# One power for both halves of a projection's head scales in a hybrid attention layer

## The chip, the cores and the metric

The kernel runs on one core of one Trainium2 chip. The metric is device time in microseconds, the median of several executions. Weights, inputs and outputs are float32; every large product is made of three float32r products (high by high, high by low, low by high).

## The reference

One decoder layer over 512 tokens with 1024 columns: a half-step SwiGLU, then two attention branches from one combined projection, then a second half-step SwiGLU. What matters for the change is that queries and keys are normalized per head before use:

```python
def rms_norm(x, g):
    y = xf * lax.rsqrt(jnp.mean(xf * xf, axis=-1, keepdims=True) + EPS)
    return (y * g).astype(x.dtype)

fq = rms_norm(fq.reshape(B, S, 8, 64), fox_q_norm)   # branch A: queries, keys
fk = rms_norm(fk.reshape(B, S, 8, 64), fox_k_norm)
dq = rms_norm(dq.reshape(B, S, 8, 64), dsa_q_norm)   # branch B: queries
dk = rms_norm(dk, dsa_k_norm)                        # one shared key head
```

Branch A is causal attention of 8 heads with a bias from cumulated forget gates. Branch B chooses for each query the 128 best keys by an indexer and attends to those, 8 query heads on one shared key and value head, with a position bias.

## The kernel before

Tokens stand in four blocks of 128 (`NT = 4`). The first feed-forward half-step takes the first 350 us, the second the last 320 us. Between them the projections are `units` of matmuls, and the attention loop runs over 16 heads `g` (0 to 7 branch A, 8 to 15 branch B) with four steps `s` each; at step `s` the scores of token block `i = 3 - s` are made, with 128(i+1) columns. `prod.run` fills TensorE between the steps with matmuls of pending units. TensorE's order is written out by hand. In this stage the orders of VectorE (DVE), ScalarE (ACT), GpSimd (POOL) and the DMA queue (SP) come from a scheduler that estimates when each operation is ready; every engine then works through its own list strictly in order.

A projection of keys or queries is one unit, `tm_proj`, of 256 columns: four heads for each of the four token blocks. Its result lies in two PSUM tiles, one for two token blocks each; these are the two halves `b` of `normed` (line 954). Six projections go through it: `fk0`, `fq0`, `fk1`, `fq1`, `dq0`, `dq1`. For each half, ACT copies PSUM to the tile `kn` (line 961, two instructions), ACT squares it into `sqh` (L857), DVE sums over the 64 columns of a head into `ss` (L859, 8 sums: two blocks of four heads), DVE scales and adds EPS (L860), POOL raises to the power -0.5 against the tile `nhalf` into `rh` (L862), and POOL multiplies `kn` by it (L964). `qk_scale` holds the middle four. `dsa_keys` calls it too, once for each token block with a single head, for the shared sparse key.

A normalized projection is used some time later: `get_k` and `get_q` transpose pairs of heads on TensorE (`ps_k`, `ps_q`, L868), and ACT and DVE take them apart into high and low parts (`kh` L851, `kl` L852, `st` L881 and L882). `ps_k`, `ps_q` and the transposed probabilities `pt` (L1209) share two PSUM banks (tag `pt`).

One step of the attention loop is, engine by engine: POOL makes the bias `b` (L1272, in branch B L1276) and masks its last 128 columns (AFFINE_SELECT, L1273); TensorE makes the score `ps_qk` (L890, L891), in one of two banks (tag `s`); DVE adds bias and score and takes the minimum (L1198, with its result `p` and `mn`); ACT takes the exponential and the row sum (L1200); DVE inverts the sum (`rs`, L1201); POOL multiplies `p` by it (L1202). The probabilities of a head are then flipped (`pt`), split by ACT into `ph` (L1213) and by DVE into `pl` (L1214), and multiplied with the values into `po` (L1219, L1220). At a head's end ACT copies `po` out twice (L1226, L1229), POOL adds the two (`o`, L1230), ACT and DVE split the sum (L1233, L1234). Values go from PSUM to `fv` by ACT (L974) and DVE (L975). Weights are split by ACT (`wh`, L138) and DVE (`wl`, L144), or, for ten of the chunks, by an accumulating DMA that POOL issues (L142).

Of the kernel before, what the change touches and what calls it, by code (L numbers as in the profile page):

```python
# [12 lines left out]
F32 = mybir.dt.float32  # L13
F32R = mybir.dt.float32r
AF = mybir.ActivationFunctionType
OP = mybir.AluOpType
AX = mybir.AxisListType
PSUM = bass.MemoryType.PSUM

P = 128  # L20
T = 512
NT = T // P
# [14 lines left out]
H = 8  # L37
DH = 64
TOPK = 128
EPS = 1e-6  # L40
# [15 lines left out]
def tile_hybrid_layer(ctx: ExitStack, tc: tile.TileContext, a: dict):  # L56
    nc = tc.nc
    V, S, G, PE = nc.vector, nc.scalar, nc.gpsimd, nc.tensor

    ctx.enter_context(tc.manual_schedule(engines={mybir.EngineType.PE}))  # L60
    const = ctx.enter_context(tc.tile_pool(name="const", bufs=1))
# [3 lines left out]
    small = ctx.enter_context(tc.tile_pool(name="small", bufs=4))  # L65
# [5 lines left out]
    def tmp_tile(name):  # L71
        return tmp.tile([P, T], F32, tag="t", name=name)
# [6 lines left out]
    for _ in range(WARM):  # L79
# [8 lines left out]
    G.memset(cpos, 0.0)  # L88
    G.affine_select(out=cpos, in_=cpos, compare_op=OP.is_ge, fill=BIG, base=0,
                    pattern=[[-1, P]], channel_multiplier=1)  # L90
    nhalf = const.tile([P, 8], F32, name="nhalf")
    G.memset(nhalf, -0.5)

    gains = const.tile([P, 3, KD], F32, name="gains")
# [671 lines left out]
    with tc.tile_pool(name="begin", bufs=1) as bp, tc.manual_schedule(  # L766
# [21 lines left out]
        for nm in ("w_gate1", "w_up1"):  # L788
            tag = next(raw_tags)
# [41 lines left out]
    with (tc.tile_pool(name="mix", bufs=1) as mp, ExitStack() as att_ctx,  # L831
# [7 lines left out]
        sd = [at.tile([P, NT, 2, DH], F32, tag="cb", bufs=2, name="sd") for _ in range(2)]  # L839
# [10 lines left out]
        def evac_split(ps, g, hi, lo):  # L850
            S.mul(hi, ps, g)  # L851
            V.scalar_tensor_tensor(lo, ps, g, hi.bitcast(F32), op0=OP.mult, op1=OP.subtract)  # L852

        def qk_scale(src, nh):

            sq = tmp_tile("sqh")
            S.activation(sq[:, :nh * DH], src, AF.Square)  # L857
            ss = small.tile([P, 8], F32, tag="ss", name="ss")
            V.tensor_reduce(ss[:, :nh], sq[:, :nh * DH].rearrange("p (h d) -> p h d", d=DH), axis=AX.X, op=OP.add)  # L859
            V.tensor_scalar(ss[:, :nh], ss[:, :nh], 1.0 / DH, EPS, op0=OP.mult, op1=OP.add)  # L860
            r = small.tile([P, 8], F32, tag="rh", name="rh")
            G.tensor_tensor(r[:, :nh], ss[:, :nh], nhalf[:, :nh], op=OP.pow)  # L862
            return r

        def transposed(cols, name):
            ps = psum.tile([P, T], F32, tag="pt", bufs=2, name=name)
            for t in range(NT):
                PE.transpose(ps[:, t * P:(t + 1) * P], cols(t), ident)  # L868
            return ps
# [83 lines left out]

        def normed(key):
            def done(ps):
                out = []
                for b in range(2):
                    kn = mp.tile([P, T], F32, tag="tn", bufs=8, name="kn")
                    kv = kn.rearrange("p (u c) -> p u c", u=2)
                    for u in range(2):  # L960
                        S.mul(kv[:, u], ps[b][:, u], rt[:, 2 * b + u:2 * b + u + 1])
                    r = qk_scale(kn, H)
                    kh = kn.rearrange("p (h d) -> p h d", d=DH)
                    G.tensor_mul(kh, kh, r[:, :, None].to_broadcast([P, H, DH]))  # L964
                    out.append(kv)
                tn[key] = out
            return done

# [128 lines left out]
        V.tensor_sub(ikl, ps, ikh.bitcast(F32))  # L1097

        def dsa_keys():
            for t in range(NT):  # L1100
                r = qk_scale(sd[0][:, t, 0], 1)
                V.tensor_scalar(sd[0][:, t], sd[0][:, t], r[:, 0:1], None, op0=OP.mult)
                S.copy(dvv[:, t, 0:64], sg[:, t, 0:64])
                V.tensor_sub(dvv[:, t, 64:128], sg[:, t, 0:64], dvv[:, t, 0:64].bitcast(F32))
            yield
            evac_split(transposed(lambda t: sd[0][:, t].rearrange("p a d -> p (a d)"), "ps_dk"), hg[:, 3:4], dkh, dkl)
# [63 lines left out]
        for h in range(H):  # L1170
# [3 lines left out]
            for i in range(1, NT):  # L1174
# [4 lines left out]
                r = tmp_tile("relu")  # L1179
# [5 lines left out]
                if h == H - 1:  # L1185
                    V.tensor_sub(sc[i][:, n - P:n], sc[i][:, n - P:n], cpos)
        later = [dsa_keys(), forget()]
        for g in later:
            next(g)
# [291 lines left out]
```

## Time and profile before

| | |
|---|---|
| median of 3 runs | 1066.27 us (1066.22 to 1066.71) |
| the profiled execution | 1065.68 us |
| its span, first to last instruction | 1064.0 us |
| TensorE busy | 1050.9 us, granted clock 1.000 |
| DVE, ACT, POOL busy | 849.9, 672.5, 258.9 us |

All times inside the program are in microseconds from the start of the span. A row of the order of time gives start, duration, engine, line, operation, output and inputs, and shapes; in brackets stands how long the engine was idle before it and which operation ended that. A row with xN merges N like instructions that follow each other. A row of the groups ends with busy time in all, the mean duration in nanoseconds, the idle time before and what ended it. What looks like full TensorE use is made of overlapping matmuls, so the small idle times are what a change of the other engines can add to or take from.

### The profile page before, as it was taken

The numbers are of one execution on the slowest core, as the hardware profiler recorded it, in microseconds if no ns is written. First come the engines' busy times: TensorE is split into PE (matmuls) and PEld (weight loads), VectorE is DVE, ScalarE is ACT, GpSimd is POOL, SyncE is SP. The second block draws the span as 40 slices with busy tenths as digits, with TensorE's granted clock in tenths as the row PEclk, the third lists the DMA queues.
The fourth block names the chain that finished last, engine by engine and source line by source line (L and its number), as shares of the span: only waits on it lengthen the run. The fifth ranks groups of instructions, "written<-read, shape, count | busy, mean of one in ns | idle before, by whom it ended". The sixth has DMA issues, their size and how long they took to land.

```text
span 1064.0 us, 19526 instructions
## 1 busy us (share of the span) xinstructions
PE 1050.9 (99%) x7438; PEld 978.0 (92%) x7438; DVE 849.9 (80%) x1400; ACT 672.5 (63%) x1120; POOL 258.9 (24%) x325
## 2 busy tenths in 40 slices
PE   9999999999999999999999999999999999999998
PEld 6889999999999899999877788888889999999998
DVE  6987888897889689976777765854987888887887
ACT  6736765765777675576867665433736765775673
POOL 1100211120122024277776653000100210111111
PEclk9999999999999999999999999999999999999999
DMA  7644654666557358633223321532543665567554
GB/s 244 150 151 115 154 155 134 143 160 174 125 126 180 99 136 201 190 92 107 80 61 119 119 70 50 162 125 78 129 160 99 148 154 156 130 158 186 127 125 129
DMA packets 57917, 143.71 MB, mean 135 GB/s; under 512 B 6616, under 2 KB 15960, under 8 KB 57824
## 3 DMA queue, kind: packets, MB, share of 16 engines
q1 hardware_dynamic: 39888, 110.22, 33.6%
q0 software_dynamic: 17792, 31.99, 17.1%
q8 instruction: 58, 0.95, 0.4%
q10 hardware_dynamic: 144, 0.26, 0.1%
q14 instruction: 35, 0.29, 0.1%
HBM read 104.94 MB, written 3.42 MB: 102 GB/s over the span
## 4 chain that ended last, share of the span: by engine, by line
PE 89%; DVE 3%; POOL 3%; ACT 2%; issue 2%; DMA 1%; SPq 0%; DVEq 0%; POOLq 0%; ACTq 0%
PE pB L149 5%; PE pB L151 5%; PE pB L150 5%; PE pA L149 3%; PE pA L151 3%; PE pA L150 3%; PE ps_f L149 3%; PE ps_f L151 3%; PE ps_f L150 3%; PE dB L151 2%; PE dB L149 2%; PE dB L150 2%; PE ps_t L149 2%; PE ps_t L151 2%; PE ps_t L150 2%; PE dA L150 2%
## 5 line engine op out<-in xcount | busy, mean ns | idle before, releaser
L118 ACT CAST wh<-s 128x1024 fp32r<-128x1024 f32 (+1 forms) x90 | 86.8, 965 | 65.6 <-PE pC L150 33.0
L125 DVE TENSOR_TENSOR wl<-s,wh 128x1024 fp32r<-128x1024 f32 (+1 forms) x90 | 100.3, 1114 | 26.9 <-ACT wh L118 26.9
L149 PE MATMUL ps_t<-wh,xh 128*128 128x256 f32 (+1 forms) x288 | 80.7, 280 | 0.0
L149 PE MATMUL pB<-tbh,wh 128*128 128x256 f32 x288 | 80.4, 279 | 0.0
L150 PE MATMUL pB<-tbl,wh 128*128 128x256 f32 x288 | 80.4, 279 | 0.0
L151 PE MATMUL ps_t<-wh,xl 128*128 128x256 f32 (+1 forms) x288 | 80.4, 279 | 0.0
L151 PE MATMUL pB<-tbh,wl 128*128 128x256 f32 x288 | 80.3, 279 | 0.0
L150 PE MATMUL ps_t<-wl,xh 128*128 128x256 f32 (+1 forms) x288 | 80.1, 278 | 0.0
L243 POOL DMA_DIRECT2D b<-gu x12 | 10.4, 864 | 222.2 <-DVE rf L443 98.4
L149 PE MATMUL ps_f<-xh,wh 128*128 128x512 f32 x152 | 60.5, 398 | 0.0
L151 PE MATMUL ps_f<-xh,wl 128*128 128x512 f32 x152 | 59.6, 392 | 0.0
L150 PE MATMUL ps_f<-xl,wh 128*128 128x512 f32 x152 | 59.6, 392 | 0.0
L1202 POOL TENSOR_SCALAR p<-p,rs 128x512 f32<-128x512 f32 (+1 forms) x64 | 40.3, 633 | 59.3 <-DVE rs L1201 57.3
L150 PEld LDWEIGHTS ps_t<-wl,xh 128*128 128x128 f32 x288 | 54.3, 188 | 0.4
L149 PEld LDWEIGHTS ps_t<-wh,xh 128*128 128x128 f32 x288 | 54.3, 188 | 0.4
L151 PEld LDWEIGHTS ps_t<-wh,xl 128*128 128x128 f32 x288 | 54.3, 188 | 0.0
L150 PEld LDWEIGHTS pB<-tbl,wh 128*128 128x128 f32 x288 | 54.1, 188 | 0.0
L151 PEld LDWEIGHTS pB<-tbh,wl 128*128 128x128 f32 x288 | 54.1, 188 | 0.0
L149 PEld LDWEIGHTS pB<-tbh,wh 128*128 128x128 f32 x288 | 54.1, 188 | 0.0
L569 POOL DMA_DIRECT2D xa<-e x20 | 23.9, 1241 | 122.5 <-ACT wh L118 102.8
L1200 ACT ACTIVATE p<-p,mn 128x512 f32<-128x512 f32 (+1 forms) x64 | 35.9, 562 | 25.1 <-DVE mn L1198 24.8
L1214 DVE TENSOR_TENSOR pl<-pt,ph 128x512 fp32r<-128x512 f32 (+1 forms) x64 | 31.0, 486 | 19.7 <-ACT ph L1213 19.0
(406 smaller groups left out, 4203.8 us busy)
## 6 DMA issues: line engine op xcount, KB each, us to landing
ra<-in_w_pair_dram SPq DMA_DIRECT2D x15, 512.0 KB, 3.9
rc<-in_w_pair_dram SPq DMA_DIRECT2D x15, 512.0 KB, 4.1
re<-in_w_pair_dram SPq DMA_DIRECT2D x12, 512.0 KB, 3.6
rf<-in_w_pair_dram SPq DMA_DIRECT2D x12, 512.0 KB, 3.5
rb<-in_w_pair_dram SPq DMA_DIRECT2D x12, 512.0 KB, 3.6
xa<-e POOLq DMA_DIRECT2D x22, 256.0 KB, 4.3
rd<-in_w_halves_dram SPq DMA_DIRECT2D x12, 384.0 KB, 3.9
ra<-in_w_halves_dram SPq DMA_DIRECT2D x9, 384.0 KB, 3.3
```

The lines of the kernel that those rows point to most:

```text
L118: S.copy(wh[:, :f], raw[:, :f])
L125: V.tensor_sub(wl[:, :f], raw[:, :f], wh[:, :f].bitcast(F32))
L149: PE.matmul(out, lh, rh, start=start, stop=False, **more)
L150: PE.matmul(out, lh, rl, start=False, stop=False, **more)
L151: PE.matmul(out, ll, rh, start=False, stop=stop, **more)
L243: G.dma_start(l, src, accum_op=OP.add)
L569: G.dma_start(xa[:, d:d + 2, HT:], t["e"][part], accum_op=OP.add)
L1200: S.activation(p, p, AF.Exp, bias=mn, scale=-1.0, accum_out=rs)
L1202: G.tensor_scalar(p, p, rs, 1.0, op0=OP.mult, op1=OP.mult)
L1214: V.tensor_sub(pl[:, sl], pt[:, sl], ph[:, sl].bitcast(F32))
```

## The change

`qk_scale` goes. In `normed`, both halves are copied, squared and summed first, into one tile `ss` of 2 x 8; one correction, one power with 16 columns and then the two multiplies follow. `dsa_keys` squares, sums, corrects and raises all four token blocks in one instruction each. `nhalf` grows from 8 to 16 columns, and the new tiles `ss2` and `rh2` have one buffer. TensorE's order is the same, and the arithmetic of each value is the same.

```diff
-    nhalf = const.tile([P, 8], F32, name="nhalf")
+    nhalf = const.tile([P, 2 * H], F32, name="nhalf")
...
-        def qk_scale(src, nh):
-            sq = tmp_tile("sqh")
-            S.activation(sq[:, :nh * DH], src, AF.Square)
-            ss = small.tile([P, 8], F32, tag="ss", name="ss")
-            V.tensor_reduce(ss[:, :nh], sq[:, :nh * DH].rearrange("p (h d) -> p h d", d=DH), axis=AX.X, op=OP.add)
-            V.tensor_scalar(ss[:, :nh], ss[:, :nh], 1.0 / DH, EPS, op0=OP.mult, op1=OP.add)
-            r = small.tile([P, 8], F32, tag="rh", name="rh")
-            G.tensor_tensor(r[:, :nh], ss[:, :nh], nhalf[:, :nh], op=OP.pow)
-            return r
...
         def normed(key):
             def done(ps):
-                out = []
+                out, kns = [], []
+                ss = small.tile([P, 2, H], F32, tag="ss2", bufs=1, name="ss")
                 for b in range(2):
                     kn = mp.tile([P, T], F32, tag="tn", bufs=8, name="kn")
                     kv = kn.rearrange("p (u c) -> p u c", u=2)
                     for u in range(2):
                         S.mul(kv[:, u], ps[b][:, u], rt[:, 2 * b + u:2 * b + u + 1])
-                    r = qk_scale(kn, H)
-                    kh = kn.rearrange("p (h d) -> p h d", d=DH)
-                    G.tensor_mul(kh, kh, r[:, :, None].to_broadcast([P, H, DH]))
+                    sq = tmp_tile("sqh")
+                    S.activation(sq, kn, AF.Square)
+                    V.tensor_reduce(ss[:, b], sq.rearrange("p (h d) -> p h d", d=DH), axis=AX.X, op=OP.add)
+                    kns.append(kn)
                     out.append(kv)
+                V.tensor_scalar(ss, ss, 1.0 / DH, EPS, op0=OP.mult, op1=OP.add)
+                r = small.tile([P, 2, H], F32, tag="rh2", bufs=1, name="rh")
+                G.tensor_tensor(r, ss, nhalf.rearrange("p (a h) -> p a h", a=2), op=OP.pow)
+                for b in range(2):
+                    kh = kns[b].rearrange("p (h d) -> p h d", d=DH)
+                    G.tensor_mul(kh, kh, r[:, b, :, None].to_broadcast([P, H, DH]))
                 tn[key] = out
             return done
...
         def dsa_keys():
+            sq = tmp_tile("sqh")
+            S.activation(sq[:, :NT * DH].rearrange("p (t d) -> p t d", t=NT), sd[0][:, :, 0], AF.Square)
+            ss = small.tile([P, 8], F32, tag="ss", name="ss")
+            V.tensor_reduce(ss[:, :NT], sq[:, :NT * DH].rearrange("p (t d) -> p t d", t=NT), axis=AX.X, op=OP.add)
+            V.tensor_scalar(ss[:, :NT], ss[:, :NT], 1.0 / DH, EPS, op0=OP.mult, op1=OP.add)
+            r = small.tile([P, 8], F32, tag="rh", bufs=2, name="rh")
+            G.tensor_tensor(r[:, :NT], ss[:, :NT], nhalf[:, :NT], op=OP.pow)
             for t in range(NT):
-                r = qk_scale(sd[0][:, t, 0], 1)
-                V.tensor_scalar(sd[0][:, t], sd[0][:, t], r[:, 0:1], None, op0=OP.mult)
+                V.tensor_scalar(sd[0][:, t], sd[0][:, t], r[:, t:t + 1], None, op0=OP.mult)
```

The scheduler answers with other orders on the four engines. In the changed file the lines of this stage have other numbers (POOL's power is L959, its multiply L962, `p` L1205, `b` L1275 and L1279, the mask L1276, `o` L1233). Three places follow.

POOL in head 3, while `fq1` is normalized: `rh` is the power, `kn` the multiply, `p` the normalized probabilities. Before:

```order
L1273 AFFINE_SELECT b<-b 128x128
L1230 TENSOR_TENSOR o<-o_5867,o 64x512
L862 TENSOR_TENSOR rh<-ss,nhalf 128x8
L1272 TENSOR_SCALAR b<-cb,ncum 128x256
L1272 TENSOR_SCALAR b<-cb,ncum 128x128
L1272 TENSOR_SCALAR b<-cb,ncum 128x512
L1202 TENSOR_SCALAR p<-p,rs 128x384
L964 TENSOR_TENSOR kn<-kn,rh 128x512
L1273 AFFINE_SELECT b<-b 128x128 x3
L862 TENSOR_TENSOR rh<-ss,nhalf 128x8
L964 TENSOR_TENSOR kn<-kn,rh 128x512
L1202 TENSOR_SCALAR p<-p,rs 128x256
```

And now:

```order
L1276 AFFINE_SELECT b<-b 128x128
L1233 TENSOR_TENSOR o<-o_5834,o 64x512
L1275 TENSOR_SCALAR b<-cb,ncum 128x256
L1275 TENSOR_SCALAR b<-cb,ncum 128x128
L1275 TENSOR_SCALAR b<-cb,ncum 128x512
L1276 AFFINE_SELECT b<-b 128x128
L1205 TENSOR_SCALAR p<-p,rs 128x384
L1276 AFFINE_SELECT b<-b 128x128 x2
L1205 TENSOR_SCALAR p<-p,rs 128x256
L959 TENSOR_TENSOR rh<-ss,nhalf 128x16
L1205 TENSOR_SCALAR p<-p,rs 128x128
L962 TENSOR_TENSOR kn<-kn,rh 128x512 x2
```

The first power and the first multiply have left the place ahead of the masks; the one power stands after `p` of 256 columns, and both multiplies after `p` of 128 columns.

ACT at the change from head 3 to head 4, where `get_k` splits the keys of the next heads. Before:

```order
L851 ACTIVATE kh<-ps_k,hg 64x512
L1213 CAST ph<-pt 128x512
L1226 COPY o<-po 64x512
L1229 COPY o_6097<-po 64x512
L851 ACTIVATE kh<-ps_k,hg 64x512
L974 ACTIVATE fv<-ps_t,rstd 128x4x64
L881 ACTIVATE st<-ps_q,gq 64x512
```

And now:

```order
L851 ACTIVATE kh<-ps_k,hg 64x512
L1216 CAST ph<-pt 128x512
L1229 COPY o<-po 64x512
L1232 COPY o_6060<-po 64x512
L971 ACTIVATE fv<-ps_t,rstd 128x4x64
L851 ACTIVATE kh<-ps_k,hg 64x512
L971 ACTIVATE fv<-ps_t,rstd 128x4x64
```

A copy of values `fv` stands ahead of the second `kh`; on DVE its partner stands ahead of the second `kl` in the same way.

POOL in head 7, while `dq1` is normalized. Before:

```order
L862 TENSOR_TENSOR rh<-ss,nhalf 128x8
L1202 TENSOR_SCALAR p<-p,rs 128x128
L964 TENSOR_TENSOR kn<-kn,rh 128x512
L1202 TENSOR_SCALAR p<-p,rs 128x512
L1272 TENSOR_SCALAR b<-cb,ncum 128x384
L1272 TENSOR_SCALAR b<-cb,ncum 128x256
L1272 TENSOR_SCALAR b<-cb,ncum 128x128
L1276 TENSOR_TENSOR b<-sc_4162,cb 128x512
L1273 AFFINE_SELECT b<-b 128x128
L1230 TENSOR_TENSOR o<-o_6881,o 64x512
L1273 AFFINE_SELECT b<-b 128x128 x2
```

And now:

```order
L959 TENSOR_TENSOR rh<-ss,nhalf 128x16
L1205 TENSOR_SCALAR p<-p,rs 128x128
L1205 TENSOR_SCALAR p<-p,rs 128x512
L962 TENSOR_TENSOR kn<-kn,rh 128x512 x2
L1275 TENSOR_SCALAR b<-cb,ncum 128x384
L1275 TENSOR_SCALAR b<-cb,ncum 128x256
L1275 TENSOR_SCALAR b<-cb,ncum 128x128
L1279 TENSOR_TENSOR b<-sc_4162,cb 128x512
L1233 TENSOR_TENSOR o<-o_6836,o 64x512
L1276 AFFINE_SELECT b<-b 128x128 x3
```

Both multiplies now stand behind `p` of 512 columns and ahead of the biases, and all three masks behind the addition `o`.

## The prediction

> **What bounds the kernel now.** I read the page first, then busy time by stretches, then the order of time on TensorE, and at each of its waits the order of time on the engine that is named there.
>
> ```profile
> span 1064.0 us, 19526 instructions
> PE 1050.9 (99%) x7438; PEld 978.0 (92%) x7438; DVE 849.9 (80%) x1400; ACT 672.5 (63%) x1120; POOL 258.9 (24%) x325
> ...
> 20.00:455.00 435.00, 434.99 (x3286) 415.59 (x3285) 372.17 (x615) 282.31 (x440) 76.00 (x86) 1.00 0.59 150
> 455.00:550.00 95.00, 90.29 (x661) 83.84 (x660) 69.39 (x171) 69.42 (x157) 73.59 (x106) 1.00 0.31 89
> 550.00:660.00 110.00, 107.24 (x554) 88.40 (x553) 78.50 (x182) 71.55 (x158) 62.95 (x74) 1.00 0.28 86
> ```
>
> The columns of the last three rows are the stretch, its length, then busy time of PE, weight loads, DVE, ACT and POOL. PE's work and its order stay as they are, so only its idle time can move: 0.01 us from 20 to 455, 4.71 us from 455 to 550, 2.76 us from 550 to 660. The rest (start and final drain) lies outside the edit. The changed operations run from 390 to 540, so what they can give directly is those 4.71 us. POOL's 24% is an average: it is busy for 73.59 of 95 us there.
>
> ```profile
> 432.03 0.28 PE L151 MATMUL ps_t<-wh,xl 128*128 128x256 f32 x1
> 432.15 0.60 PE L868 MATMUL ps_q<-ident,kn 128*128 128x128 f32 x4
> ...
> 482.73 0.50 PE L890 MATMUL ps_qk<-kh,st 128*128 128x512 f32 x1 [0.58 <-DVE mn L1198]
> 486.32 0.66 PE L1209 MATMUL pt<-ident,p 128*128 128x128 f32 x4 [0.32 <-POOL p L1202]
> 490.41 0.55 PE L1209 MATMUL pt<-ident,p 128*128 128x128 f32 x3 [0.31 <-DVE kl L852]
> ...
> 517.03 0.55 PE L1209 MATMUL pt<-ident,p 128*128 128x128 f32 x3 [1.06 <-DVE kl L852]
> ...
> 538.23 0.66 PE L1209 MATMUL pt<-ident,p 128*128 128x128 f32 x4 [1.07 <-POOL p L1202]
> ...
> 544.79 0.22 PE L890 MATMUL ps_qk<-kh,st 128*128 128x128 f32 x1
> 547.80 0.38 PE L1220 MATMUL po<-pl,fv 128*128 128x256 f32 x1 [0.33 <-DVE pl L1214]
> ```
>
> A matmul is drawn 0.28 long but the next starts 0.12 later (432.03, 432.15), so a stall costs about 0.16 more than the idle printed. I count 0.74, 0.48, 0.47, 1.22, 1.23 and 0.49 us for the six.
>
> **The price of one power.**
>
> ```profile
> L862 POOL TENSOR_TENSOR rh<-ss,nhalf 128x8 f32<-128x8 f32 x12 | 21.9, 1828 | 12.5 <-DVE ss L860 12.3
> L964 POOL TENSOR_TENSOR kn<-kn,rh 128x512 f32<-128x512 f32 x12 | 13.4, 1118 | 0.2
> L185 POOL TENSOR_TENSOR rstd<-v,nhalf 128x4 f32<-128x4 f32 x3 | 3.4, 1143 | 15.3 <-DVE v L183 15.2
> L862 POOL TENSOR_TENSOR rh<-ss,nhalf 128x1 f32<-128x1 f32 x4 | 2.5, 861 | 0.0
> L860 DVE TENSOR_SCALAR ss<-ss 128x8 f32<-128x8 f32 x12 | 3.1, 257 | 0.1
> ...
> 482.68 1.66 POOL L862 TENSOR_TENSOR rh<-ss,nhalf 128x8 f32<-128x8 f32 x1
> ```
>
> No row has 16 columns. Undisturbed, 8 cost 1.66 and 4 cost 1.14 (mean), 0.13 a column. 16 then cost 1.66 + 8 x 0.13 = 2.7 us (my value). The bounds are 1.66 (flat) and 3.32 (two for the price of two). Each projection saves 0.6 us of POOL, six of them 3.7. The sparse keys' four powers (2.5) become one of 1.14, and their four squares, sums and corrections become one each. That saving, and the six corrections dropped on DVE (about 0.26 each), lie up to 455 for the first two projections and the sparse keys, where PE idles 0.01 us and PE is the cover. I count them 0; later corrections sit beside DVE's own waits. With the cover gone they could give at most their own 2.5 us, which nothing on PE asks for.
>
> What the edit really moves is order: no power starts before the second half's sum, and two multiplies (1.12 each, mean) follow it in one piece.
>
> **First query projection (418 to 432): counted 0.**
>
> ```profile
> 424.91 1.66 POOL L862 TENSOR_TENSOR rh<-ss,nhalf 128x8 f32<-128x8 f32 x1 [1.84 <-DVE ss L860]
> ...
> 428.73 0.92 POOL L142 DMA_DIRECT2D wl<-ra  x1 [1.03 <-ACT wl L141]
> ```
>
> POOL's new order puts this weight transfer ahead of both multiplies, and it waits for ACT until 428.7. The power (424.9 to 427.6) is done by then. The multiplies run behind the transfer, which ends at 429.65: 2 x 1.12 gives 431.9, and PE takes them at 432.15 and after. It fits by 0.25 us; what comes later than that PE pays in full.
>
> **Head 3, POOL: -1.22 us.**
>
> ```profile
> 476.12 2.71 POOL L862 TENSOR_TENSOR rh<-ss,nhalf 128x8 f32<-128x8 f32 x1 [0.17 <-DVE ss L860]
> 478.84 1.55 POOL L1272 TENSOR_SCALAR b<-cb,ncum 128x256 f32<-128x256 f32 x3
> ...
> 481.92 0.80 POOL L1273 TENSOR_SCALAR_AFFINE_SELECT b<-b 128x128 f32<-128x128 f32 x3
> ...
> 485.45 1.49 POOL L1202 TENSOR_SCALAR p<-p,rs 128x256 f32<-128x256 f32 x3
> ...
> 482.24 0.43 DVE L1198 CUSTOM_DVE_ANT_0 p<-ps_qk,b 128x256 f32<-128x256 f32 x1 [1.83 <-POOL b L1273]
> 482.80 1.22 DVE L144 TENSOR_TENSOR wl<-rc,wh 128x1024 fp32r<-128x1024 f32 x1
> ```
>
> PE waits at 482.73 for DVE's score, the score for the mask (481.92), and the mask stands behind power, biases and multiply. In the new order the first power and multiply are gone from there: biases 476.1 to 477.7, mask by 478.0, over 4 us early. The 0.74 goes. Next, the wait at 486.32 is for p of 128 columns. The new queue is p256, power, p128, then the multiplies. With the power from about 481.5 to 484.2, p128 is ready at 484.6, and PE, 0.74 earlier, asks at about 485.2. The 0.48 goes too.
>
> [...]
>
> **Head 3 to 4, ACT: +0.5 us.**
>
> ```profile
> 489.59 0.47 ACT L974 ACTIVATE fv<-ps_t,rstd 128x256 fp32r<-128x256 f32 x1
> ...
> 489.60 0.76 DVE L852 SCALAR_TENSOR_TENSOR kl<-ps_k,hg,kh 64x512 fp32r<-64x512 f32 x1 [1.22 <-ACT kh L851]
> ```
>
> PE's transposes at 490.41 wait for the bank that this kl frees. The new order runs a value copy fv (0.47) ahead of that kh. Chain and demand both come 1.22 us earlier, so the wait grows by the copy: 0.47 to about 0.97.
>
> **Head 5, DVE: +0.2 us.**
>
> ```profile
> 515.18 0.67 DVE L860 TENSOR_SCALAR ss<-ss 128x8 f32<-128x8 f32 x1
> 516.22 0.76 DVE L852 SCALAR_TENSOR_TENSOR kl<-ps_k,hg,kh 64x512 fp32r<-64x512 f32 x1 [0.37 <-ACT kh L851]
> 517.01 0.56 DVE L1198 CUSTOM_DVE_ANT_0 p<-ps_qk,b 128x384 f32<-128x384 f32 x1
> ```
>
> The score of 517.01 now stands ahead of the kl of 516.22: 515.85 + 0.56 = 516.41, so kl starts 0.2 late and the 1.22 at 517.03 becomes 1.4.
>
> **Head 7, POOL: +0.8 us.**
>
> ```profile
> 536.15 1.66 POOL L862 TENSOR_TENSOR rh<-ss,nhalf 128x8 f32<-128x8 f32 x1
> 537.81 0.36 POOL L1202 TENSOR_SCALAR p<-p,rs 128x128 f32<-128x128 f32 x1
> ...
> 539.17 1.71 POOL L1202 TENSOR_SCALAR p<-p,rs 128x512 f32<-128x512 f32 x1
> 540.86 1.41 POOL L1272 TENSOR_SCALAR b<-cb,ncum 128x384 f32<-128x384 f32 x3
> ...
> 543.49 0.29 POOL L1273 TENSOR_SCALAR_AFFINE_SELECT b<-b 128x128 f32<-128x128 f32 x1
> 543.86 1.29 POOL L1230 TENSOR_TENSOR o<-o,o 64x512 f32<-64x512 f32 x1
> ...
> 543.81 0.56 DVE L1198 CUSTOM_DVE_ANT_0 p<-ps_qk,b 128x384 f32<-128x384 f32 x1 [0.45 <-POOL b L1273]
> ```
>
> The score of 128 columns no longer waits behind biases, so the power can start near 534.8 and p128 ends at 537.9 in place of 538.17: -0.3. Behind it now come p512 (1.71 here, about 0.7 inside the 1.49 of the three at 485.45), two multiplies (2.2), the biases (540.86 to 543.49: 2.6), the addition o (1.29), and only then the mask (0.29), which stood ahead of o before. That is 545.0 to 546.0; I take the middle, 545.5. The score of 384 columns (0.56) then ends at 546.1. Its PSUM bank is the one for the matmul of 544.79 (two banks in turn), now asked for at 544.5: +1.6. The pl that ended the wait at 547.80 moves ahead of this score on DVE: -0.5. Net +0.8.
>
> **Sum.** -1.22 + 0.5 + 0.2 + 0.8 = +0.3 us on a span of 1064.0. That execution took 1065.68 us, 1.7 more than its span and 0.6 under the median of 1066.27. Against the median I forecast 1066.6 us; this case's own range is 1065.3 to 1067.9 (head 7 alone is worth 0.5 either way, the copy and the first query projection 0.3 each).
>
> **Rivals.** (a) Faster: POOL was the hidden cause of other waits. For it: 73.59 of 95 us busy, and 5.1 us of work leave. If the power costs 1.66, p128 at head 7 comes before its demand and the whole 1.23 goes, in place of 0.3. If a third of the remaining 2.76 idle up to 660 goes with it, and the mask comes 0.8 earlier, the sum is 0.3 - 0.9 - 0.9 - 0.8 = -2.3: 1064.0. Against: those later waits name DVE, and no changed operation runs there. (b) Slower: the two multiplies in one piece hold the normalizations and the masks. It decides where the mask at head 7 comes after 546.0. With p512 at 1.71 and the pair held up by the same 1.0 that p512 lost, the mask is at 547.0 and PE stalls 3.1 there, 1.5 more than counted; the same piece ahead of p128 at head 6 costs up to 1.0 near 525. Sum +2.8: 1069.1. For it: POOL has no gap there; against: head 6 has DVE's slack. (c) The power of 16 costs 3.32, so POOL saves nothing: p128 and the mask at head 7 come 0.6 later, +0.7: 1067.3.
>
> **How the numbers follow.** Forecast 0.52, (a) 0.16, (b) 0.19, (c) 0.13. A change of 0.2% (2.1 us) is about what a measurement tells from none: forecast and (c) are within it, 0.65; faster 0.16, slower 0.19. The range 1063.9 to 1069.0 takes in (a) and (c) and stops just short of (b).
>
> **What would show it.** Right: one power of about 2.7 us per projection, no idle near 482 and 486, over 0.6 near 490, a new wait on the 128-column score near 545. Wrong: idle from 455 to 660 under 5.4 or over 9.6 us, or idle appearing before 455.

## The result, and the profile after

| | before | after |
|---|---|---|
| median | 1066.16 us | 1081.1 us |
| the profiled execution | 1065.68 us | 1079.76 us |
| its span | 1064.0 us | 1078.1 us |

The changed kernel is slower: ratio 1.0144, 95% interval 1.0134 to 1.0154. The forecast was 1066.6.

The page of the changed kernel, and its busy time by the same stretches as before (PE, weight loads, DVE, ACT, POOL, then the granted clock):

```profile
span 1078.1 us, 19508 instructions
PE 1064.8 (99%) x7438; PEld 991.3 (92%) x7438; DVE 848.5 (79%) x1388; ACT 672.5 (62%) x1117; POOL 254.3 (24%) x316
...
20.00:455.00 435.00, 434.76 (x3233) 415.01 (x3232) 365.71 (x585) 277.29 (x428) 72.04 (x78) 1.00 0.59 148
455.00:550.00 95.00, 90.97 (x688) 85.70 (x686) 68.99 (x171) 69.95 (x154) 70.11 (x99) 1.00 0.31 93
550.00:660.00 110.00, 105.59 (x544) 87.15 (x544) 79.39 (x192) 72.52 (x164) 64.61 (x80) 1.00 0.28 85
```

PE's idle time from 455 to 660 is 4.03 + 4.41 = 8.44 us, 1.0 more than before. That is not where 14 us went. PE is *busy* for 13.9 us more (1064.8 against 1050.9) with the same 7438 matmuls in the same order and the same clock. The first row tells it already: 3233 matmuls begin between 20 and 455, where 3286 did.

Two stretches of 50 us in the feed-forward stages, in which no instruction was edited, before:

```profile
150.00:200.00 50.00, 50.00 (x430) 1.00 0.62 158
850.00:900.00 50.00, 50.00 (x429) 1.00 0.63 165
```

and after:

```profile
150.00:200.00 50.00, 50.00 (x420) 1.00 0.61 153
850.00:900.00 50.00, 50.00 (x419) 1.00 0.67 166
```

PE is fully busy at clock 1.00 in both, and gets through 2.3% fewer matmuls. Compare the start of the same matmul, the nth in both traces: the changed kernel is 6.2 us late at the end of the first feed-forward (355 us), 6.1 at 448, 6.4 at 647 behind the attention stage, 7.1 at 780 and 14.1 at the end. The attention stage, the only one the prediction worked on, adds 0.3 us. The rest is a slower pitch, the time from the start of one matmul to the start of the next.

By the form of one product (minimum, median and maximum of the drawn duration, then first and last start), before:

```profile
L150 PE MATMUL pB<-tbl,wh x288: 277/280/281, 80.3 to 1030.8; 128*128 128x256 f32 x144
L149 PE MATMUL ps_out<-mh,wh x64: 389/389/389, 685.2 to 728.0; 128*128 128x512 f32 x64
```

and after:

```profile
L150 PE MATMUL pB<-tbl,wh x288: 279/284/287, 80.8 to 1044.2; 128*128 128x256 f32 x144
L149 PE MATMUL ps_out<-mh,wh x64: 394/394/395, 691.7 to 735.0; 128*128 128x512 f32 x64
```

A duration is drawn about 163 ns longer than the pitch (280 for 116.7). The same products of the same shapes are 4 and 5 ns longer, and the last `pB` starts 13.4 us later. From here on "pitch" is the mean of start to start over consecutive matmuls of one product, gaps over 160 ns (256 columns) or 330 ns (512 columns) left out.

### The profile page after: what moved, and what is told of

It is laid out like the page before. It is cut to its first block, busy times and chain, and to the rows that moved or that the text cites. A ratio compares the mean times of both kernels' runs of the same rounds, so it can differ in the third digit from the quotient of the medians.

```text
span 1078.1 us, 19508 instructions
## 1 busy us (share of the span) xinstructions
PE 1064.8 (99%) x7438; PEld 991.3 (92%) x7438; DVE 848.5 (79%) x1388; ACT 672.5 (62%) x1117; POOL 254.3 (24%) x316
## 4 chain that ended last, share of the span: by engine, by line
PE 88%; DVE 5%; ACT 2%; DMA 2%; issue 2%; POOL 1%; SPq 0%; POOLq 0%; DVEq 0%; ACTq 0%
PE pB L150 5%; PE pB L149 5%; PE pB L151 5%; PE pA L150 3%; PE pA L149 3%; PE pA L151 3%; PE ps_f L149 3%; PE ps_f L151 3%; PE ps_f L150 3%; PE ps_t L149 3%; PE ps_t L151 3%; PE ps_t L150 3%; PE dB L150 2%; PE dB L151 2%; PE dB L149 2%; PE dA L150 2%
## 5 line engine op out<-in xcount | busy, mean ns | idle before, releaser
L1205 POOL TENSOR_SCALAR p<-p,rs 128x512 f32<-128x512 f32 (+1 forms) x64 | 37.0, 581 | 61.8 <-DVE rs L1204 55.9
```

The costliest lines, as they stand in the source:

```text
L1205: G.tensor_scalar(p, p, rs, 1.0, op0=OP.mult, op1=OP.mult)
```

## The experiments

**What could touch the feed-forward.** The edit changes two sizes. `nhalf` is 32 bytes per partition larger, in the first pool. The pool of small tiles had 4 buffers of `ss` and 4 of `rh` (256 bytes); it now has `ss2`, `rh2`, 4 of `ss` and 2 of `rh` (64 + 64 + 128 + 64 = 320). Pools stand behind each other in the order const, inputs, weights, scratch, small, and then the feed-forward's or the attention's own pools. So inputs and weights move by 32 bytes and everything behind the small pool by 96. The kernel has traces of someone having cared about such places: an unused `hp.tile([P, 8], F32, name="pad")` in the feed-forward's second pool (L208), and weight tiles that start 56 or 8 columns into their buffer (L502, L135).

From the addresses in the two programs I took for each matmul the start of the moving operand minus the start of the stationary one, modulo 256 bytes. I call this the distance. In the kernel before, all 5304 matmuls with 256 columns of the feed-forward and of `ps_t` have distance 32, and 1440 of those with 512 have distance 0. After, 4248 of the first have 96 and 576 of the second (`pd`, `ps_out` and others) have 64. The other 1056 (the 768 of `ps_t`, and some of `dB` and `dD`), whose operands both lie ahead of the small pool, stay at 32, and their pitch stays at 117 ns.

**Shift everything by 32 bytes.**

```diff
-    nhalf = const.tile([P, 8], F32, name="nhalf")
+    nhalf = const.tile([P, 16], F32, name="nhalf")
```

> The kernel before with only the constant tile of halves made 16 columns wide instead of 8 (32 bytes a partition more in the first pool), so that every pool behind it, inputs, weights and activations alike, lies 32 bytes further on; the powers stay as they were. Theory A (the loss comes from how far the moving operand of a matmul lies from the stationary one, in bytes modulo 128, which this leaves as it was): 1065.5 to 1067, no change. Theory B (the loss comes from the place of a tile by itself): 1072 to 1081. Theory C (the loss comes from the merged powers and their order): no change, as A.

1066.22 us against 1066.44, ratio 0.9998 (0.9989 to 1.0007). A common shift of all operands by 32 bytes does nothing: theory B, in which the place of a tile by itself counts, falls for this shift.

**Shift only the pools behind the small tiles, by 64 bytes.** No instruction differs from the kernel before.

```diff
     small = ctx.enter_context(tc.tile_pool(name="small", bufs=4))
+    small.tile([P, 16], F32, tag="pad", bufs=1, name="pad")
```

> The kernel before with an unused tile of 16 columns (64 bytes a partition) in the pool of small tiles, so that only the pools of the feed-forward and of the attention lie 64 bytes further on from weights and inputs. No instruction differs. In it 4248 of the matmuls with 256 columns go from a distance of 32 bytes (moving minus stationary, modulo 128) to 96, as in the changed kernel. Theory A: 4248 at about 3 ns each, and some with 512 columns at 2 to 3 ns, so 1079 to 1081, with a pitch of 119 to 121 ns for the 256-column matmuls of the feed-forward. Theory C: 1066 to 1067.

1081.41 us, ratio 1.0142 (1.0127 to 1.0156): the whole loss, from an unused tile. In this kernel lines are one higher:

```profile
150.00:200.00 50.00, 50.00 (x420) 1.00 0.61 152
850.00:900.00 50.00, 50.00 (x419) 1.00 0.67 165
L151 PE MATMUL pB<-tbl,wh x288: 279/282/286, 80.8 to 1045.0; 128*128 128x256 f32 x144
L150 PE MATMUL ps_out<-mh,wh x64: 394/394/394, 692.3 to 735.6; 128*128 128x512 f32 x64
```

The rows are those of the changed kernel. Theory C, that the merged powers cost the time, falls.

**The changed kernel with its first pool as it was.** The power reads the 8 columns twice by a broadcast.

```diff
-    nhalf = const.tile([P, 2 * H], F32, name="nhalf")
+    nhalf = const.tile([P, 8], F32, name="nhalf")
...
-                G.tensor_tensor(r, ss, nhalf.rearrange("p (a h) -> p a h", a=2), op=OP.pow)
+                G.tensor_tensor(r, ss, nhalf[:, None, :].to_broadcast([P, 2, H]), op=OP.pow)
```

> The changed kernel with the constant tile of halves back at 8 columns (the power reads it twice by a broadcast), so that the first pool has its old size and only the pool of small tiles is larger, by 64 bytes. Theory A: the distances are those of the changed kernel, 1079 to 1082. Theory B (the first 32 bytes): 1066 to 1068. Theory C: 1079 to 1082.

1082.11 us, ratio 1.0143 (1.0129 to 1.0156). The wider `nhalf` is innocent; only the small pool counts.

**The changed kernel, shifted on to 128 bytes.** The same unused tile of 16 columns as above, in the changed kernel.

> The changed kernel with an unused tile of 16 columns (64 bytes) in the pool of small tiles, so that the feed-forward and attention pools lie 128 bytes, not 64, further from the weights than before. All of the change's instructions are kept. Theory A: the distances modulo 128 are those of the kernel before, so the loss goes: 1066.6, as the prediction's sum has it, 1065.5 to 1068. Theories B and C: 1079 to 1082.

1073.47 us, ratio 1.0068 (1.0056 to 1.008): half of the loss remains, so a distance modulo 128 is not the whole rule.

```profile
L151 PE MATMUL pB<-tbl,wh x288: 277/280/282, 81.4 to 1036.9; 128*128 128x256 f32 x144
L150 PE MATMUL ps_out<-mh,wh x64: 392/395/398, 687.6 to 731.7; 128*128 128x512 f32 x64
```

Theory A as it stood, with a period of 128, had all of the loss gone, and missed. At distance 160 the products with 256 columns are nearly as fast as at 32 (117.6 against 116.9 ns, x 4248 = 3.0 us), but those with 512 columns (`pd`, `ps_out`, `ps_bb`) are slower at 128 than at 0 (233.3 against 226.7, x 576 = 3.8 us). That is 6.8 of the 7.0 us measured. Counted in the same way, the changed kernel loses 4248 x (119.8 - 116.9) = 12.3 us and 576 x (229.0 - 226.7) = 1.3 us; with the 0.3 of the attention stage it makes 13.9 of 14.1.

**The changed kernel at the old distances.** One of its tiles has buffers that are never used; two fewer make the small pool as large as before. Every engine's order is that of the changed kernel.

```diff
-            ss = small.tile([P, 8], F32, tag="ss", name="ss")
+            ss = small.tile([P, 8], F32, tag="ss", bufs=2, name="ss")
```

> The changed kernel with two buffers instead of four for the sparse keys' sums (only one is ever in use), so that the pool of small tiles is as large as before the change and the feed-forward and attention pools stand where they stood. On every engine the order of instructions is that of the changed kernel. Theory A, now with the distance counted modulo 256 (the shift by 128 gave back half of the loss, not all): the loss goes, 1066.6 by the prediction's sum, 1065.3 to 1067.9. Theory C (something in the merge itself costs the feed-forward time): 1079 to 1082.

1066.61 us, ratio 1.0002 (0.9993 to 1.0011). The loss is gone, and this is what the edit is worth without its side effect: nothing that can be measured.

**Its two parts apart,** both at the old distances. The projections alone (the two new tiles in the pool of constants, which shifts all operands together):

> The kernel before with the merged power for the projections alone (the sparse keys keep four powers), its two new tiles laid in the pool of constants, so that no distance between operands changes. All terms of the prediction's sum come from this part: 1066.6 (+0.3), with the stalls near 482 and 486 gone and a new one of about 1.6 near 546. Rival (the sparse keys' merge carries part of it): 1067.3 or more, or 1065.3 or less.

1067.86 us, ratio 1.0008 (0.9999 to 1.0017). The sparse keys alone:

> The kernel before with one power for the sparse keys of all token blocks alone, the pools of their old sizes. The prediction counts it 0: 1066.3 (1065.7 to 1067). Rival: the 2.5 us of powers on GpSimd were worth something to a later unit, 1064 to 1065.5.

1066.41 us, ratio 1.0 (0.999 to 1.0009). Counting the sparse keys as 0 is borne out. The projections' median lies above the bound named for the rival, but the interval holds the forecast of +0.3 as well as +1.8; it doesn't tell them apart.

**The pitch at each distance.** One kernel, in which the weights of the halved feed-forward products start at sixteen places in turn, and those of the eight output chunks at eight:

```diff
-        wh = wpool.tile([P, 1088], F32R, tag="wh", name="wh")[:, at:]
+        wh = wpool.tile([P, 1088], F32R, tag="wh", name="wh" + s)[:, at:]
...
-                    return split_w(src, n_w, at=56, between=between)
+                    return split_w(src, n_w, at=200 + 8 * next(sweep), between=between)
...
-                wh, wl = load_w(a["w_out"][d], KD, P)
+                wh, wl = load_w(a["w_out"][d], KD, P, to=d)
```

(The 200 is taken off again inside `split_w`; it only marks these tiles, and `s` is their letter. `wl` likewise.)

> The kernel before, with the weight tiles of the halved feed-forward products started at 0, 32, 64 ... 480 bytes in turn (names whA to whP) instead of always at 224, and those of the eight output chunks at 0, 32 ... 224 bytes (whQ to whX). The same instructions otherwise. It measures the pitch of the matmuls at each distance (moving minus stationary, in bytes). Theory A (only the distance modulo 256 decides): for 256 columns 116.7 ns at 32, 119 to 120 at 96, 117.3 to 118.5 at 160, and names eight letters apart (A and I, B and J ...) alike within 0.5 ns; for 512 columns 227 at 0, 230 at 64, 230 to 238 at 128. Rival A2 (a longer period decides): names eight letters apart differ by 2 ns or more. Rival B (the place of the weights by itself): the same at all starts a multiple of 64 bytes apart. In all some 1 to 3 us over the kernel before.

The tiles' own rows, for starts A, C, D and F (distances 0, 192, 160, 96):

```profile
L154 PE MATMUL dB<-al,whA x12: 278/283/284, 225.9 to 869.5; 128*128 128x256 f32 x12
L154 PE MATMUL dB<-al,whC x12: 276/276/286, 137.2 to 325.1; 128*128 128x256 f32 x12
L154 PE MATMUL dB<-al,whD x12: 282/283/285, 874.1 to 1061.9; 128*128 128x256 f32 x12
L154 PE MATMUL dB<-al,whF x12: 279/280/287, 329.7 to 973.1; 128*128 128x256 f32 x12
```

Mean pitch in ns, about 85 to 100 matmuls with 256 columns per entry, 23 with 512:

| distance | 0 | 32 | 64 | 96 | 128 | 160 | 192 | 224 |
|---|---|---|---|---|---|---|---|---|
| 256 columns, starts 0 to 224 | 119.4 | 117.8 | 117.8 | 119.4 | 118.5 | 120.2 | 113.6 | 118.2 |
| 256 columns, starts 256 to 480 | 119.5 | 117.7 | 117.8 | 119.6 | 118.4 | 120.1 | 113.9 | 118.5 |
| 512 columns | 226.7 | 233.3 | 229.3 | 233.4 | 233.5 | 233.9 | 233.4 | 233.1 |

Starts 256 bytes apart agree within 0.3 ns, so 256 bytes is a period, and rivals A2 and B fall. Only the weights moved here, and only the moving operands in the run with the unused tile; the pitch changed in both, and did not when both moved together. So it goes with the distance. Two of theory A's figures missed: 116.7 was expected at 32 and 118.5 at most at 160, where 117.8 and 120.2 came; more on this below. The kernel as a whole took 1067.23 us in its one run. The kernel before stood at the best distance for its 512-column products and at a good one, not the best, for those with 256.

With the same matmuls in the same order the pitch of the 256-column products runs from 113.6 ns at distance 192 to 120.2 at 160. Why one distance is slower than another is not shown.

**All 256-column products at 192.** The changed kernel at its old small pool, and the kernel before, each with the weights started elsewhere in their buffers; the order on every engine stays.

```diff
-        wh, wl = (w[:, at:at + f] for w in (wh, wl) for at in [8 if m > P else 0])
+        wh, wl = (w[:, at:at + f] for w in (wh, wl) for at in [48 if m > P else 0])
...
-                    return split_w(src, n_w, at=56, between=between)
+                    return split_w(src, n_w, at=16, between=between)
```

(and `at=24` in place of 0 in the seven other calls of `split_w` for 256-column products)

> The changed kernel with the old size of the small pool (as in the run where its loss was gone, 1066.61), and the weight tiles of all 256-column products started elsewhere in their buffers, so that the distance of the 5304 matmuls is 192 bytes modulo 256 instead of 32. Instructions and their order are the same. Theory A: the sweep had 113.7 ns at 192 and 116.8 at 32, 5304 x 3.1 = 16.4 us, so 1050 (1048 to 1054). Rival D (TensorE's pitch is not what the feed-forward takes its time from: another engine, or the loads, pace it, and faster matmuls only turn into idle time): 1058 to 1066, with idle time of TensorE in place of the gain.

> The kernel before with the same starts of the weight tiles (distance 192 in place of 32), without the merged powers. Theory A: 1050 (1048 to 1054), and against the changed kernel with the same starts a difference of the size of the prediction's sum, 0.3 us (under 1.5 either way). Rival E (with a faster TensorE the attention stage has less slack, and the merged powers are worth something): over 2 us slower than the changed kernel with the same starts.

1060.84 us with the merged powers (ratio 0.9934, 0.9911 to 0.9957) and 1058.26 without (0.9923, 0.9908 to 0.9938). Both beat the kernel before: their medians are 5.8 and 8.4 us under the 1066.65 beside them. That is a third to a half of the 16.4 us of theory A (which counts from 116.8 at 32, near the 116.9 of the kernel before; the sweep had 117.8 there). Both times lie in rival D's range, but rival D falls all the same, as PE has no idle time in place of the rest:

```profile
250.00:300.00 50.00, 50.00 (x444) 1.00 0.55 135
1000.00:1050.00 50.00, 50.00 (x426) 1.00 0.55 128
```

These are two stretches of the version without the merged powers. Both are fully busy at clock 1.00, yet one has 444 matmuls and the other 426. Taken by stretches of 5 us, its pitch in the feed-forward is 113.3 or 117.8 ns, and holds there for 20 to 100 us on end before it changes to the other. The mean is 115.1, and 5304 x (115.1 - 116.9) = -9.5 us. With the merged powers the stretches fall elsewhere:

```profile
250.00:300.00 50.00, 50.00 (x427) 1.00 0.52 132
1000.00:1050.00 50.00, 50.00 (x431) 1.00 0.62 133
```

So at 192 there are two steady pitches. Distance 32 has two as well, closer together. The kernel before, taken in the same way, runs at 116.7 ns in most of the feed-forward and at 117.8 from 250 to 310 us; beside the 430 matmuls of 150 to 200 us stands

```profile
250.00:300.00 50.00, 50.00 (x427) 1.00 0.55 136
```

Within these traces the pitch changes almost only where the `p` products of one group of weights give way to the `d` products, or these to the next group's `p`. The two versions at 192 can't be ranked: their medians differ by 2.6 us, more than the 1.5 that was expected, but their intervals overlap. Rival E is not shown, since the version without the merged powers was not the slower one.

**The sweep once more,** in steps of 16 bytes (`4 * next(sweep)`), after these two:

> The sweep once more with steps of 16 bytes: weight tiles of the halved feed-forward products at 0, 16, 32 ... 240 bytes (names whA to whP, distance 0, 240, 224, 208, 192, 176 ... 16 modulo 256); the eight output chunks as before. Theory A (the distance alone decides, as in the first sweep): the multiples of 32 bytes repeat within 0.5 ns of what they had (119.5 at 0, 118.4 at 224, 113.7 at 192, 120.2 at 160, 118.5 at 128, 119.5 at 96, 117.8 at 64), and those between lie between or near their neighbours. Rival F (192 has two pitches, 113.3 and 117.8, and which of them a stretch falls into is not set by the distance): the tile at 192 (whE) reads 115 to 118 this time.

| distance | 0 | 16 | 32 | 48 | 64 | 80 | 96 | 112 |
|---|---|---|---|---|---|---|---|---|
| pitch, ns | 119.5 | 117.4 | 116.8 | 116.7 | 117.8 | 118.2 | 119.5 | 119.3 |

| distance | 128 | 144 | 160 | 176 | 192 | 208 | 224 | 240 |
|---|---|---|---|---|---|---|---|---|
| pitch, ns | 118.4 | 119.4 | 118.7 | 118.9 | 113.5 | 117.8 | 118.3 | 118.3 |

The repeat holds within 0.5 ns but for 32 and 160, which differ by 1.0 and 1.5 between the sweeps. At 32 the products had 117.8 in the first sweep and mostly 116.6 in the second, the two pitches that the kernel before has at this distance. So the distance is not alone; the products at 32 and 160 came behind products at other distances in the second sweep than in the first, but what decides was not tested. At 192 every product of both sweeps was near the fast pitch (means of 113.3 to 114.6), and each came behind a product at another distance; rival F's reading did not come. What decides between the two pitches in a kernel that has 192 throughout stays open. This kernel took 1069.74 us in its one run, against 1066.7.

**Does the stream collide with the next weights or its own?** The high and the low weights at different distances:

```diff
-        wl = wpool.tile([P, 1088], F32R, tag="wl", name="wl")[:, at:]
+        wl = wpool.tile([P, 1088], F32R, tag="wl", name="wl")[:, at if low is None else low:]
...
-                    return split_w(src, n_w, at=56, between=between)
+                    return split_w(src, n_w, at=16, between=between, low=24)
```

> The kernel before with the high weight parts of the halved feed-forward products started so that their distance is 192, and the low parts so that it is 160. In each triple (high weights with high values, high weights with low values, low weights with high values) the first matmul streams while high weights stand in the array and high weights are loaded for the next; the second streams while the low weights are loaded; the third streams over low weights while high ones are loaded. Theory G (what collides is the stream with the load of the next weights): the second of each triple is slow (about 120 ns), the first and third fast (about 113.6). Rival H (the stream and the weights it is multiplied with): the third is slow, the first and second fast. Neither: all three alike, about 115 to 118.

In the trace of the kernel before, the weight loads (0.19 us each) start together with the matmuls of a triple (0.28 us each): high, low, high weights beside the first, second and third.

```profile
159.87 0.19 PEld L150 LDWEIGHTS dC<-al,wh 128*128 128x128 f32 x1
159.99 0.19 PEld L151 LDWEIGHTS dC<-ah,wl 128*128 128x128 f32 x1
160.10 0.19 PEld L149 LDWEIGHTS dC<-ah,wh 128*128 128x128 f32 x1
```

```profile
159.87 0.28 PE L149 MATMUL dC<-ah,wh 128*128 128x256 f32 x1
159.99 0.28 PE L150 MATMUL dC<-al,wh 128*128 128x256 f32 x1
160.10 0.28 PE L151 MATMUL dC<-ah,wl 128*128 128x256 f32 x1
```

The three kinds of matmul have 118.0, 118.4 and 119.9 ns (498, 498 and 419 of them), and the kernel took 1069.22 us in its one run, against 1065.62. Theory G falls, as the second is not the slow one. The third is the slowest, as rival H has it, but the first two are not fast. This is what each would have by its own distance if 192 were in its slower pitch (117.8) and 160 near the 120.2 of the first sweep; it is also what a slowing of all three by the one slow partner would look like. The run can't tell these apart, and what collides stays open.

## Why the prediction was wrong

**The step that failed** stands in its first part: "PE's work and its order stay as they are, so only its idle time can move", with "the rest (start and final drain) lies outside the edit". The work and its order did stay. Its pitch did not: it went from 116.9 to 119.8 ns in 4248 matmuls and from 226.7 to 229.0 in most of 576 others, and 13.6 of the 14.1 us are there. The prediction put this term at nothing. The sizes of `nhalf`, `ss2` and `rh2` stood in the diff, and were read for what they do in the attention stage alone. No row of the trace before shows a tile's address; the pad of 8 columns and the odd starts in the code were the hint.

For the same reason the signs named for a wrong forecast didn't ring: PE's idle time from 455 to 660 is 8.44 us, inside the band of 5.4 to 9.6. Up to 455 it went from 0.01 to 0.24, but that one gap is at 54 us, in the first feed-forward, where no edited operation runs. They watched idle time only.

**The sum itself, term by term,** in the changed kernel. PE's waits in the stretches concerned:

```profile
495.45 0.55 PE L1212 MATMUL pt<-ident,p 128*128 128x128 f32 x3 [0.88 <-DVE kl L852]
...
521.82 0.55 PE L1212 MATMUL pt<-ident,p 128*128 128x128 f32 x3 [1.06 <-DVE kl L852]
...
543.17 0.66 PE L1212 MATMUL pt<-ident,p 128*128 128x128 f32 x4 [1.08 <-POOL p L1205]
...
551.80 0.33 PE L879 MATMUL ps_qk<-kh,st 128*128 128x128 f32 x1 [1.86 <-DVE mn L1201]
```

- *Price of the power, 2.7:* 2.92 (2915 to 2933 ns in all six), nearer to the upper bound of 3.32 than was taken. So 16 columns cost 1.76 times the 1.66 of 8.

```profile
L959 POOL TENSOR_TENSOR rh<-ss,nhalf x6: 2915/2924/2933, 413.0 to 539.8; 128x16 f32<-128x16 f32 x6
L1103 POOL TENSOR_TENSOR rh<-ss,nhalf x1: 1330/1330/1330, 399.2 to 399.2; 128x4 f32<-128x4 f32 x1
```

- *First query projection, 0:* right. The two multiplies end at 437.84, and PE takes them at 438.26.
- *Head 3, POOL, -1.22:* right. PE has no such wait from 484 to 495; the waits for `mn` and for `p` are gone.
- *Head 3 to 4, ACT, +0.5:* right. The wait for `kl` has grown from 0.31 to 0.88 as printed, +0.57.
- *Head 5, DVE, +0.2:* 0. The wait is 1.06 as before. The score does stand ahead of the `kl`, but ends at 520.73, and the `kl` of 521.01 still waits for ACT's `kh`, 0.28.
- *Head 7, POOL, +0.8:* mechanism right, size low. The wait for `p` stayed (1.08 against 1.07, -0.3 expected; the power is 0.22 dearer than counted). The new wait for the 128-column score came, 1.86 as printed and about 2.0 in all, where 1.6 was counted. The wait at 547.80 before is gone, -0.49.

Together -1.22 + 0.57 + 2.0 - 0.49 = +0.9 in place of +0.3. By the starts of the same matmuls in both traces two places that the prediction didn't list give 0.5 back: 0.18 at the matmul that started at 497.33 before, and 0.31 at the one of 573.36, whose wait of 0.37 for DVE shrinks to 0.05. That makes +0.4, near the 0.3 that the stage as a whole adds. With the distances restored the kernel takes 1066.61, so the forecast would have stood had the tiles kept their places. That the number would have fit so well is in part luck: head 7 cost 0.7 more than counted, and head 5 and the two places not listed made up for it.

The head 7 wait can be followed on POOL, now ahead of the mask:

```profile
539.84 2.92 POOL L959 TENSOR_TENSOR rh<-ss,nhalf 128x16 f32<-128x16 f32 x1 [0.63 <-DVE ss L957]
542.75 2.01 POOL L1205 TENSOR_SCALAR p<-p,rs 128x128 f32<-128x128 f32 x2
544.73 2.04 POOL L962 TENSOR_TENSOR kn<-kn,rh 128x512 f32<-128x512 f32 x2
546.76 1.40 POOL L1275 TENSOR_SCALAR b<-cb,ncum 128x384 f32<-128x384 f32 x3
548.13 1.30 POOL L1279 TENSOR_TENSOR b<-sc,cb 128x512 f32<-128x512 f32 x1
549.51 1.26 POOL L1233 TENSOR_TENSOR o<-o,o 64x512 f32<-64x512 f32 x1
550.85 0.79 POOL L1276 TENSOR_SCALAR_AFFINE_SELECT b<-b 128x128 f32<-128x128 f32 x3
```

It is the queue that the prediction listed, and 11 us pass from the power's start to the mask.

**The subtraction beside the power.** In head 3 DVE's subtraction for the low weights (`wl`, L144) runs beside POOL's power. Before, the one of 482.80 started inside the power of 482.68 to 484.34; it took 1.22 us, the median of its like, and the power 1.66. In the changed kernel the subtraction started inside the longer power, ran beside it for 1.0 us and ended 0.25 us after it, and both took their usual time (1.22 and 2.92):

```profile
487.28 2.92 POOL L959 TENSOR_TENSOR rh<-ss,nhalf 128x16 f32<-128x16 f32 x1
```

```profile
489.23 1.22 DVE L144 TENSOR_TENSOR wl<-rc,wh 128x1024 fp32r<-128x1024 f32 x1
```

In two other places one of a pair that overlapped took longer. The subtraction of 527.44 started inside the second of two multiplies, and took 2.05:

```profile
526.36 2.04 POOL L962 TENSOR_TENSOR kn<-kn,rh 128x512 f32<-128x512 f32 x2
```

```profile
527.44 2.05 DVE L144 TENSOR_TENSOR wl<-ra,wh 128x1024 fp32r<-128x1024 f32 x1 [0.93 <-ACT wh L138]
```

And the power that the prediction shows at 476.12 took 2.71 us, where the one of 482.68 took 1.66. It began 0.03 us after the start of a subtraction, in the kernel before:

```profile
476.09 1.23 DVE L144 TENSOR_TENSOR wl<-rb,wh 128x1024 fp32r<-128x1024 f32 x1
```

What made these two longer is not shown.

**The rivals.** None of them was the one. (b), slower by the pair of multiplies, had the sign but not the place: masks and PE waits account for under 1 us.

## What to carry to other kernels

In this kernel's pools a diff that changes the size or the number of buffers of any tile moves every tile in the pools behind it; before costing its instructions, list which operands of the main matmul loop shift against each other. When a kernel is bound by TensorE at 99%, read the number of matmuls per 50 us as well as the idle time: a slower pitch shows as full use (here 50.00 of 50 us busy with 430 matmuls and with 420). And an edit that slows stages it doesn't touch is best tried with an unused tile of the same size alone, or with the size given back.

## What the runs showed of the hardware

That the pitch of float32r matmuls, each with its own weight load (7438 of each on the page), depends on the distance of the two operands in SBUF was not expected: 113.5 to 120.2 ns with 256 columns, 226.7 to 233.9 with 512, with a period of 256 bytes (for 256 columns, within 0.3 ns) and different best distances (192, and 0). Nor was it that one distance can have two pitches that hold for tens of microseconds (113.3 and 117.8 at 192, 116.7 and 117.8 at 32). In 50 us the number of matmuls tells them apart (444, 430 and 420 in the rows above, for 113.3, 116.7 and about 120 ns), while the clock reads 1.00 in each.

One smaller thing: behind the long wait of head 7 the granted clock can dip. In the changed kernel at its old distances:

```profile
540.00:545.00 5.00, 3.08 (x15) 0.97 0.20 52
545.00:550.00 5.00, 5.00 (x18) 0.69 0.01 3
550.00:560.00 10.00, 10.00 (x54) 1.00 0.25 72
```

5 us at 0.69 cost about 1.5 us (an estimate, 5 x 0.31, if the matmuls slow with the clock). The profiled execution of the changed kernel itself has the same wait and no dip, so it is not certain to follow; its cause wasn't tested.
